# A constant product written into each free PSUM bank ahead of the real products of RWKV's blocks, retention and GLA

## The chip, the cores and the metric

The kernel runs on one core of a Trainium2 chip. A core has a matrix engine (TensorE: PE in the profile, PEld for its weight loads), VectorE (DVE), ScalarE (ACT), GpSimd (POOL), SyncE (SP, which only issues and waits here) and 16 DMA engines. The metric is the device time of one execution in microseconds. The kernel before takes 2861.12 us (median of 3 runs, 2857.55 to 2868.86).

## The reference

One encoder layer over 2048 tokens of width 1024, in float32: a norm, one input projection, four token mixers of width 256 side by side (retention, RWKV-7, a linear recurrence, gated linear attention), an output projection with a residual, a router that gives each of 16 experts its best 256 tokens, the experts' feed-forward products, and a last norm. The mixers are bidirectional. Cut to what the change touches:

```
def _retention_chunked(q, k, v, log_gamma):           # and the same on flipped inputs
    scores = einsum('bnihd,bnjhd->bnhij', qc, kc) * dmask
    y_intra = einsum('bnhij,bnjhe->bnihe', scores, vc)
    state = state * chunk_decay + kv_i                 # scan over chunks
    y_cross = einsum('bnihd,bnhde,hi->bnihe', qc, prev, xi)
...
def step(S, inp):                                      # RWKV-7, per token
    sa = einsum('bhvk,bhk->bhv', S, -kk_t)
    S = S * w_t + sa * (kk_t * a_t) + v_t * k_t
    y = einsum('bhvk,bhk->bhv', S, r_t)
...
def _gla_chunked(q, k, v, log_alpha):
    scores = where(lower, einsum('bnihk,bnjhk->bnhij', q_dec, k_dec), 0.0)
    y_intra = einsum('bnhij,bnjhv->bnihv', scores, v)
    S = S * dec + kv_i                                 # scan over chunks
```

## The kernel before

The program runs in stages. Until about 836 us the input projection runs, and beside it the linear recurrence and the first half of RWKV (`rwkv_a`: decays, and the inverses of the small triangular systems). From 836 to about 1450 us three streams share the engines, and this is the stage that the change touches: the rest of RWKV (`rwkv_rest`), retention and GLA. Then come the output projection of the remaining blocks (to about 1630 us), the choice of tokens (`top_k`) and the 16 experts (to the end).

RWKV's rest goes over 16 blocks of 128 tokens in both directions. For each block and direction `rwkv_prep` makes the block's matrices in six steps: transposes of two tensors (L606, then L615, with the identity as one operand), the products L628 (64 partitions, two banks), L639, L648, and L656 in two halves of two heads each. ScalarE or VectorE takes each bank to SBUF before the next step. One block later `rwkv_chain` does the recurrence (L672, two products of four heads per block and direction). Retention goes over 16 blocks of 128 tokens: transposes (L938), scores (L952), and the block's output (L960 and L963, accumulated in one bank), besides state updates (L909) in a first pass over all blocks and again in each. GLA goes over 16 blocks: two score products (L1217) and the output (L1233, L1234, L1236 in one bank), after a first pass that makes its decays.

Every product writes a PSUM bank from `bank`. PSUM has eight banks in three pools: four for RWKV's rest (stream 0), two for retention (stream 1), two for GLA (stream 2). A bank is handed to the next product when the last reader of its former contents is done. When RWKV's blocks are through, stream 0 goes on with the weights of the output projection (`out_weights`, L43 and L44) and with its first four blocks (`out_proj`, L129).

The streams are generators that a function weaves together, in shares of 100 for RWKV's rest, 56 for retention and 68 for GLA. This gives every instruction its priority. A scheduler then fixes the order on each engine ahead of time, by its own model of times: it takes an instruction when its operands are there and, if the instruction is the first to write a tile, when a buffer of the pool is free. On the chip each engine runs its list in that order.

In the profile a product of two float32 operands appears as two records, and a transpose as one.

Of the kernel before, what the change touches and what calls it, by code (L numbers as in the profile page):

```python
# [8 lines left out]
BF16 = mybir.dt.bfloat16  # L9
# [8 lines left out]
P = 128  # L18
# [27 lines left out]

def bank(g, which=None, shape=(P, 512)):
    return g.ps[g.stream if which is None else which].tile(list(shape), F32, name="bank", tag="bank")


def rstd_of(g, pool, ss, n, scale, eps, name):
# [510 lines left out]
def turn(ring):  # L562
    ring[1] += 1
    return ring[0][(ring[1] - 1) % len(ring[0])]
# [20 lines left out]
def rwkv_prep(g, dr, b, loaded, res):  # L585

    nc, c = g.nc, g.c
    ld, q1, ti = loaded  # L590
    q0 = turn(g.q0)
    z, v = ([ld[:, HALF * q + o:HALF * q + o + P] for q in range(2)] for o in (384, 512))
    bk = [[ld[:, HALF * q + 192 - 128 * e:HALF * q + 320 - 128 * e] for e in range(2)] for q in range(2)]
    R = g.bp.tile([P, NH, P], F32, name="R", tag="R")
    mv = [g.mp.tile([P, NH, C], F32, name=f"mv{e}", tag=f"mv{e}") for e in range(2)]
    g.mv[dr, b] = mv
    H = [slice(0, 64), slice(64, 128)]

    def qh(x):
        return x.rearrange("p (q h) c -> p q h c", q=2)  # L600

    p1 = bank(g)
    for q in range(2):
        for e in range(2):
            o = (2 * q + e) * P
            nc.tensor.transpose(p1[:, o:o + P], bk[q][e], c["ident"])  # L606
    p1 = p1.rearrange("p (q e h c) -> p q e h c", q=2, e=2, h=2)
    for e in range(2):
        for s, q in ((H[e], q0), (H[1 - e], q1)):
            nc.scalar.activation(out=qh(q[s, :, e, H[1 - e]]), in_=p1[s, :, e], func=AF.Copy)  # L610
    yield
    p2 = bank(g)
    for i, x in enumerate((z, v)):
        for q in range(2):
            nc.tensor.transpose(p2[:, i * 256 + q * P:i * 256 + (q + 1) * P], x[q], c["ident"])  # L615
    p2 = p2.rearrange("p (i h c) -> p i h c", i=2, h=NH)
    for e in range(2):
        nc.scalar.activation(out=R[H[e], :, H[e]], in_=p2[H[e], 0], func=AF.Copy)
        nc.scalar.activation(out=mv[e][H[1 - e]], in_=p2[H[1 - e], 1], func=AF.Copy)
    yield  # L620
    rd = turn(g.rd)
    for k in range(2):
        nc.vector.tensor_copy(out=rd[H[k], :, k], in_=ld[H[k]].rearrange("p (u t) -> p u t", t=320)[:, :, 0:C])
    pss = [bank(g) for _ in range(2)]
    for q in range(2):
        for k in range(2):
            ks = ld[H[k], HALF * q:HALF * q + 384].rearrange("p (u t) -> p u t", t=C)[:, 1::3]
            nc.tensor.matmul(pss[k][:, q * P:(q + 1) * P], lhsT=z[q][H[k]], rhs=ks, start=True, stop=True)  # L628
    for k in range(2):
        pv = pss[k][:, 0:256].rearrange("p (q e t) -> p q e t", q=2, e=2)  # L630
        for e in range(2):
            s = H[e]
            nc.vector.tensor_tensor(out=R[s, k::2, H[1 - e]], in0=pv[s, :, 1 - e], in1=c["m_bm"][s, dr, None, :].broadcast_to([64, 2, C]), op=OP.mult)
    yield
    ps = bank(g)
    for q in range(2):
        for e in range(2):
            o = (2 * q + e) * P
            nc.tensor.matmul(ps[:, o:o + P], lhsT=bk[q][e], rhs=rd[:, 2 * q + 1 - e], start=True, stop=True)  # L639
    pv = ps.rearrange("p (q e h t) -> p q e h t", q=2, e=2, h=2)  # L640
    for e in range(2):
        for s, q in ((H[e], q0), (H[1 - e], q1)):
            nc.vector.tensor_tensor(out=qh(q[s, :, e, H[e]]), in0=pv[s, :, e], in1=c["m_in"][s, dr, None, None, :].broadcast_to([64, 2, 2, C]), op=OP.mult)
    yield

    ps = bank(g)
    for h in range(NH):
        nc.tensor.matmul(ps[:, h * P:(h + 1) * P], lhsT=ti[:, h], rhs=R[:, h], start=True, stop=True)  # L648
    X = g.bp.tile([P, NH, P], F32, name="X", tag="X")
    nc.scalar.activation(out=X, in_=ps.rearrange("p (h c) -> p h c", h=NH), func=AF.Copy)  # L650
    yield
    E = g.ep.tile([P, NH, 2, P], F32, name="E", tag="E")
    for h2 in range(2):
        ps = bank(g)
        for h in range(2):
            nc.tensor.matmul(ps[:, h * 256:(h + 1) * 256], lhsT=X[:, 2 * h2 + h, :], rhs=q0[:, 2 * h2 + h].rearrange("p e c -> p (e c)"),  # L656
                             start=True, stop=True)
        s = slice(2 * h2, 2 * h2 + 2)
        nc.vector.tensor_tensor(out=E[:, s].rearrange("p h e c -> p (h e c)"), in0=q1[:, s].rearrange("p h e c -> p (h e c)"), in1=ps, op=OP.subtract)
        yield  # L660
    res[dr, b] = E
# [222 lines left out]
def retention(g):  # L884
# [44 lines left out]
    for j in range(NB // 4):  # L929
        y4 = g.sh.tile([P, 4, 256], F32, name="rt_y4")  # L930
        for b in range(4 * j, 4 * j + 4):
            ld = pool.tile([P, 768], F32, name="rt_ld")
            nc.sync.dma_start(out=ld, in_=g.tm[b, :, 0:768])
            vv = ld[:, 512:768]
            rot = rotate(g, pool, b, ld[:, 0:512], 2 * NH).rearrange("p h t -> p (h t)")
            ps = bank(g)
            for q in range(4):
                nc.tensor.transpose(ps[:, q * P:(q + 1) * P], rot[:, q * P:(q + 1) * P], c["ident"])  # L938
            pq = ps[:, 0:256].rearrange("p (q t) -> p q t", q=2)
            qd = turn(qds)  # L940
            for k in range(2):
                nc.scalar.activation(out=qd[halves[k], :, k], in_=pq[halves[k]], func=AF.Copy)
            qT = pool.tile([P, 2, P], F32, name="rt_qT")
            nc.scalar.activation(out=qT, in_=pq, func=AF.Copy)
            qs = pool.tile([P, 2, 2, P], F32, name="rt_qs")
            nc.gpsimd.tensor_tensor(out=qs, in0=qT[:, None].broadcast_to([P, 2, 2, P]), in1=g.rxi, op=OP.mult)
            kT = pool.tile([P, 2, P], F32, name="rt_kT")
            nc.scalar.activation(out=kT, in_=ps[:, 256:512].rearrange("p (q t) -> p q t", q=2), func=AF.Copy)
            sd = [diag(S[0]), diag(SB[:, b])]
            ps = bank(g)  # L950
            for q in range(2):
                nc.tensor.matmul(ps[:, q * 256:(q + 1) * 256], lhsT=kT[:, q], rhs=qd[:, q].rearrange("p k t -> p (k t)"), start=True, stop=True)  # L952
            sT = pool.tile([P, NH, P], F32, name="rt_sT")
            nc.vector.tensor_tensor(out=sT, in0=ps.rearrange("p (h t) -> p h t", h=NH), in1=g.rdt, op=OP.mult)
            yield
            ps = bank(g)
            for q in range(2):
                o = ps[:, q * P:(q + 1) * P]
                for e in range(2):
                    nc.tensor.matmul(o, lhsT=qs[:, e, q], rhs=sd[e][:, q].rearrange("p k v -> p (k v)"), start=(e == 0), stop=False)  # L960
                for h in (2 * q, 2 * q + 1):
                    s = slice(h * HD, (h + 1) * HD)
                    nc.tensor.matmul(ps[:, s], lhsT=sT[:, h], rhs=vv[:, s], start=False, stop=(h == 2 * q + 1))  # L963
            nc.scalar.activation(out=y4[:, b - 4 * j], in_=ps[:, 0:256], func=AF.Copy)
            if b + 1 < NB:
                state(0, b, rot[:, 256:512].rearrange("p (h t) -> p h t", h=NH), vv)
            yield
        head_norm(g, g.sh, y4.rearrange("p b (h v) -> p (b h) v", v=HD), 16, True, EPS)
        yield
        gated_out(g, g.sh, y4, j, 6, g.w_ret_gn, 0)  # L970
        yield
# [110 lines left out]
def gla(g):  # L1082
# [114 lines left out]
    for j in range(NJ):  # L1197
# [7 lines left out]
        for b in range(GB * j, GB * j + GB):  # L1205
# [5 lines left out]
            pss = []  # L1211
            for e in range(2):
                qx = pool.tile([P, NH, P], F32, name="gl_qx", tag="gl_qx")
                nc.gpsimd.tensor_tensor(out=qx, in0=o[:, 0, e, None, s].broadcast_to([P, NH, P]),
                                        in1=c["gl_hq"][:, :, None].broadcast_to([P, NH, P]), op=OP.mult)
                ps = bank(g)
                nc.tensor.matmul(ps, lhsT=o[:, 1, e, s], rhs=qx.rearrange("p h t -> p (h t)"), start=True, stop=True)  # L1217
                pss.append(ps.rearrange("p (h t) -> p h t", h=NH))

# [3 lines left out]
            for e in range(2):  # L1223
                p, r = H64[e], H64[1 - e]
# [3 lines left out]
            for p in H64:  # L1228
                nc.gpsimd.tensor_tensor(out=sT[p, :, p], in0=sT[p, :, p], in1=t[p], op=OP.add)
            yield  # L1230
            ps = bank(g)
            y = ps[:, 0:256]
            nc.tensor.matmul(y, lhsT=o[:, 0, 0, s], rhs=sx[0], start=True, stop=False)  # L1233
            nc.tensor.matmul(y, lhsT=o[:, 0, 1, s], rhs=sx[1], start=False, stop=False)  # L1234
# [591 lines left out]
```

## Time and profile before

| | us |
|---|---|
| median of 3 runs | 2861.12 |
| the profiled execution | 2858.58 |
| its span, first to last instruction | 2856.6 |
| PE busy | 2594.7 (91%) |
| PEld busy | 2321.6 (81%) |
| DVE busy | 1746.1 (61%) |
| ACT busy | 1392.3 (49%) |
| POOL busy | 711.5 (25%) |
| mean granted TensorE clock | 0.947 |

Busy time of PE includes the time that a product is in flight, so consecutive products overlap in it, and the distance of their starts tells better what one costs. The granted clock is the share of TensorE's full speed that the chip gave. It has two levels, 2.4 GHz (1.0) and 1.2 GHz (0.5), and a mean between them is a mixture over time.

### The profile page before, as it was taken

What the parts mean: (1) busy time and instruction counts of PE and PEld (TensorE: products, weight loads), DVE (VectorE), ACT (ScalarE), POOL (GpSimd) and SP (SyncE); (2) the same over time, 40 slices, a digit from 0 to 9 for tenths busy, and PEclk for the clock granted to TensorE, in tenths of its full rate; (3) what the DMA queues carried; (4) which work ended last, traced back from release to release, by engine and by line L of the source; (5) the groups of instructions that cost most, each with busy time, mean ns of one, the idle gap of its engine ahead of it and who ended that gap; (6) DMA issues with size and microseconds to landing.
All of it is one profiled execution on the core that took longest, in us unless ns stands there. A gap on an engine that the chain in (4) does not pass through costs nothing.

```text
span 2856.6 us, 47428 instructions
## 1 busy us (share of the span) xinstructions
PE 2594.7 (91%) x18433; PEld 2321.6 (81%) x18433; DVE 1746.1 (61%) x3415; ACT 1392.3 (49%) x2348; POOL 711.5 (25%) x771
## 2 busy tenths in 40 slices
PE   6989998989888888886979859999999999999997
PEld 5866787768767777774767659999999999999987
DVE  4454567766887667788443475555555555566564
ACT  4366555435434676555533334444444444455453
POOL 0011115443524454347433200000000000000121
PEclk9999999999988889997989979999999999999999
DMA  8735554675446544446344346666666666789873
GB/s 304 278 101 190 182 164 151 203 231 166 136 122 177 161 153 148 145 127 190 107 143 171 127 147 206 205 206 205 206 205 205 205 206 206 228 289 298 266 238 140
DMA packets 474015, 538.40 MB, mean 188 GB/s; under 512 B 129952, under 2 KB 411584, under 8 KB 473024
## 3 DMA queue, kind: packets, MB, share of 16 engines
q1 hardware_dynamic: 461984, 492.12, 53.3%
q0 software_dynamic: 11808, 43.26, 5.8%
q8 instruction: 145, 2.38, 0.3%
q14 instruction: 78, 0.64, 0.1%
HBM read 392.17 MB, written 145.23 MB: 188 GB/s over the span
## 4 chain that ended last, share of the span: by engine, by line
PE 53%; DVE 5%; DMA 4%; ACT 3%; issue 2%; POOL 1%; SPq 0%; POOLq 0%; ACTq 0%; DVEq 0%
PE bank L129 43%; DMA rt_ld<-tm 1%; PE bank L656 1%; PE bank L1500 1%; PE bank L639 1%; DMA fn_x<-acc,x_idx 1%; PE bank L628 1%; PE bank L672 1%; PE bank L1481 1%; PE bank L648 1%; DVE tk_j L1395 0%; PE bank L1217 0%; PE bank L1323 0%; PE bank L960 0%; PE bank L952 0%
## 5 line engine op out<-in xcount | busy, mean ns | idle before, releaser
L44 DVE TENSOR_TENSOR x_wl<-x_st,x_wh 128x2048 fp32r<-128x2048 f32 x192 | 439.5, 2292 | 306.3 <-ACT x_wh L43 305.9
L129 PE MATMUL bank<-x_xh,x_wh 128*128 128x256 f32 x2048 | 580.2, 285 | 2.9 <-ACT x_wh L43 2.8
L129 PE MATMUL bank<-x_xl,x_wh 128*128 128x256 f32 x2048 | 577.4, 283 | 0.0
L129 PE MATMUL bank<-x_xh,x_wl 128*128 128x256 f32 x2048 | 572.2, 283 | 1.1 <-DVE x_wl L44 1.1
L43 ACT ACTIVATE x_wh<-x_st 128x2048 fp32r<-128x2048 f32 x192 | 367.0, 1913 | 106.7 <-PE bank L129 96.6
L129 PEld LDWEIGHTS bank<-x_xh,x_wh 128*128 128x128 f32 x2048 | 393.2, 192 | 3.6 <-ACT x_wh L43 3.2
L129 PEld LDWEIGHTS bank<-x_xl,x_wh 128*128 128x128 f32 x2048 | 393.3, 192 | 0.0
L129 PEld LDWEIGHTS bank<-x_xh,x_wl 128*128 128x128 f32 x2048 | 389.9, 192 | 1.5 <-DVE x_wl L44 1.5
L129 PE MATMUL bank<-x_wh,x_hh 128*128 128x256 f32 x1024 | 290.1, 285 | 4.8 <-ACT x_hh L43 4.8
L129 PE MATMUL bank<-x_wl,x_hh 128*128 128x256 f32 x1024 | 291.2, 285 | 0.0
L129 PE MATMUL bank<-x_wh,x_hl 128*128 128x256 f32 x1024 | 289.8, 284 | 0.0
L1626 POOL DMA_INDIRECT acc<-x_os,x_idx x30 | 48.9, 1631 | 926.8 <-ACT x_os L1560 899.0
L129 PE MATMUL bank<-h_hi,w_hi 128*128 128x512 f32 x576 | 238.5, 417 | 20.1 <-DVE o_cm L1676 13.8
L129 PE MATMUL bank<-h_lo,w_hi 128*128 128x512 f32 x576 | 240.0, 417 | 0.0
L129 PE MATMUL bank<-h_hi,w_lo 128*128 128x512 f32 x576 | 235.6, 409 | 0.0
L129 PEld LDWEIGHTS bank<-x_wh,x_hh 128*128 128x128 f32 x1024 | 196.6, 193 | 5.0 <-ACT x_hh L43 5.0
L129 PEld LDWEIGHTS bank<-x_wl,x_hh 128*128 128x128 f32 x1024 | 197.4, 193 | 0.0
L129 PEld LDWEIGHTS bank<-x_wh,x_hl 128*128 128x128 f32 x1024 | 197.2, 193 | 0.0
L129 PE MATMUL bank<-w_hi,h_hi 128*128 128x256 f32 (+1 forms) x512 | 156.4, 306 | 14.6 <-DVE o_tm L1676 11.8
L129 PEld LDWEIGHTS bank<-h_hi,w_hi 128*128 128x128 f32 x576 | 112.5, 196 | 56.3 <-DVE o_cm L1676 16.4
L129 PE MATMUL bank<-w_lo,h_hi 128*128 128x256 f32 (+1 forms) x512 | 149.4, 292 | 0.0
L129 PE MATMUL bank<-w_hi,h_lo 128*128 128x256 f32 (+1 forms) x512 | 148.8, 291 | 0.0
(457 smaller groups left out, 5490.2 us busy)
## 6 DMA issues: line engine op xcount, KB each, us to landing
x_st<-in_exp_w_gate_dram SPq DMA_DIRECT2D x64, 1024.0 KB, 8.4
x_st<-in_exp_w_up_dram SPq DMA_DIRECT2D x64, 1024.0 KB, 8.9
x_st<-in_exp_w_down_dram SPq DMA_DIRECT2D x64, 1024.0 KB, 5.5
w_st<-in_w_in_dram SPq DMA_DIRECT2D x20, 1024.0 KB, 6.7
rw_sp<-sp SPq DMA_DIRECT2D x16, 1280.0 KB, 4.6
bld<-rw_sp SPq DMA_DIRECT2D x32, 640.0 KB, 4.1
ld<-rw_cm SPq DMA_DIRECT2D x14, 899.5 KB, 6.1
cm<-o_cm SPq DMA_DIRECT2D x40, 256.0 KB, 2.8
```

The source lines that it names most:

```text
L43: g.nc.scalar.activation(out=hi, in_=src, func=AF.Copy)
L44: (g.nc.gpsimd if pool else g.nc.vector).tensor_tensor(out=lo, in0=src, in1=hi.bitcast(F32), op=OP.subtract)
L129: g.nc.tensor.matmul(out, lhsT=lhs[a][:, k, lsl], rhs=rhs[b][:, k, rsl], start=(k + i == 0 and out is outs[0]), stop=(3 * k + i == 3 * nk ...
L628: nc.tensor.matmul(pss[k][:, q * P:(q + 1) * P], lhsT=z[q][H[k]], rhs=ks, start=True, stop=True)
L639: nc.tensor.matmul(ps[:, o:o + P], lhsT=bk[q][e], rhs=rd[:, 2 * q + 1 - e], start=True, stop=True)
L648: nc.tensor.matmul(ps[:, h * P:(h + 1) * P], lhsT=ti[:, h], rhs=R[:, h], start=True, stop=True)
L656: nc.tensor.matmul(ps[:, h * 256:(h + 1) * 256], lhsT=X[:, 2 * h2 + h, :], rhs=q0[:, 2 * h2 + h].rearrange("p e c -> p (e c)"), start=True ...
L672: nc.tensor.matmul(ps[:, h, :], lhsT=E[:, h, e, :], rhs=mv[e][:, h, :], start=True, stop=True)
L1481: nc.tensor.matmul(ps[:, 2 * s:2 * s + 2], lhsT=oh[:, i, s * P:(s + 1) * P], rhs=tok[:, i], start=(i == 0), stop=(i == NB - 1))
L1500: nc.tensor.transpose(ps[:, m * CAP + s * P:m * CAP + (s + 1) * P], xs[:, s, (k + m) * P:(k + m + 1) * P], c["ident"])
L1626: g.nc.gpsimd.indirect_dma_start(out=dst, out_offset=bass.IndirectOffsetOnAxis(ap=idx[:, s:s + 1], axis=0), in_=t[:, s], in_offset=None, **kw)
```

## The change

A new function `full` puts one product into a bank before the bank goes to its real user: the first 128 columns of the identity matrix, read as bf16, against 512 columns of the same matrix, over all 128 partitions and all 512 columns of the bank. Nothing reads its result: each real product starts its sum anew and writes over it. It stands ahead of L606, L615, the first of the two banks of L628, L639, L648 and both halves of L656 in RWKV's blocks; ahead of L938, L952 and L960 in retention; and ahead of both L1217 and of L1233 in GLA. The recurrence (L672), the state updates (L909), the first pass of GLA and the output projection are left as they are. Line numbers after the new function are higher by 8.

```
+def full(g, ps):
+    i = g.c["ident"].bitcast(BF16)
+    g.nc.tensor.matmul(ps.rearrange("p (a b) -> p a b", a=2), lhsT=i[:, 0:P], rhs=i[:, None, :].broadcast_to([P, 2, 2 * P]), start=True, stop=True)
+    return ps
...
@@ rwkv_prep
-    p1 = bank(g)
+    p1 = full(g, bank(g))
...
-    p2 = bank(g)
+    p2 = full(g, bank(g))
...
-    pss = [bank(g) for _ in range(2)]
+    pss = [full(g, bank(g)), bank(g)]
...
-    ps = bank(g)
+    ps = full(g, bank(g))
     for q in range(2):
         for e in range(2):
...
-    ps = bank(g)
+    ps = full(g, bank(g))
     for h in range(NH):
         nc.tensor.matmul(ps[:, h * P:(h + 1) * P], lhsT=ti[:, h], rhs=R[:, h], start=True, stop=True)
...
     for h2 in range(2):
-        ps = bank(g)
+        ps = full(g, bank(g))
...
@@ retention: three times, ahead of the transposes, the scores and the output
-            ps = bank(g)
+            ps = full(g, bank(g))
...
@@ gla: ahead of each score product and of the output
-                ps = bank(g)
+                ps = full(g, bank(g))
```

The scheduler places 320 such products on PE; 245 of them stand directly ahead of their own real product, and 75 have other products in between. The other products change places too. Two places show it.

The first is PE in RWKV's third block, from the products L648 (R times ti, both directions) to the end of L656 (q0 times X, both directions). Before:

```order
L648 MATMUL bank_8124<-R_7940,ti0_7184 128x128 x4
L648 MATMUL bank_8131<-R_7952,ti1_7185 128x128 x4
L909 MATMUL bank_7819<-rt_ld_7810,rt_kz_7817 128x128 x2
L656 MATMUL bank_8161<-q00_7166,X_8129 128x256 x2
L656 MATMUL bank_8166<-q01_7167,X_8136 128x256 x2
L656 MATMUL bank_8243<-q00_7166,X_8129 128x256 x2
L656 MATMUL bank_8247<-q01_7167,X_8136 128x256 x2
```

The same place of the change, the part with L656 (now L664; L55 is the constant product, whose weight load is a row of its own):

```order
L55 LDWEIGHTS c_ident_84
L55 MATMUL bank_8199<-c_ident_84 128x512
L664 MATMUL bank_8199<-q00_7166,X_8166 128x256 x2
L55 LDWEIGHTS c_ident_84
L55 MATMUL bank_8205<-c_ident_84 128x512
L55 LDWEIGHTS c_ident_84
L55 MATMUL bank_8283<-c_ident_84 128x512
L664 MATMUL bank_8283<-q00_7166,X_8166 128x256 x2
L664 MATMUL bank_8205<-q01_7167,X_8174 128x256 x2
L55 LDWEIGHTS c_ident_84
L55 MATMUL bank_8288<-c_ident_84 128x512
L664 MATMUL bank_8288<-q01_7167,X_8174 128x256 x2
```

Four constant products have come in, the bank of the second direction's first half (8205) is taken two products before its real use, and the halves of the first direction now follow each other.

The second place is PE at the end of RWKV's recurrence, the last product of L672 and what stands around it. Before:

```order
L938 MATMUL bank_10856<-c_ident_84,rt_a1_10851 128x128 x4
L1153 MATMUL bank_10818<-c_ident_84,gl_p_10297 128x128 x2
L672 MATMUL bank_12780<-mv1_12551,E_12697 128x64 x4
L672 MATMUL bank_12786<-mv0_12562,E_12702 128x64 x4
L952 MATMUL bank_10873<-rt_qd0_7362,rt_kT_10867 128x256 x2
L1159 MATMUL bank_10818<-gl_v_10299,gl_kt_10821 32x64 x8
```

And of the change (L672 is now L680, L938 is L946, L952 is L960):

```order
L680 MATMUL bank_13100<-mv1_12857,E_13013 128x64 x4
L946 MATMUL bank_11884<-c_ident_84,rt_a1_11879 128x128 x4
L680 MATMUL bank_13106<-mv0_12869,E_13019 128x64 x4
L960 MATMUL bank_11902<-rt_qd1_7369,rt_kT_11896 128x256 x2
```

Counted over the whole list, 10 of retention's 16 score products and 8 of GLA's 16 blocks stand ahead of that last product before, and 13 and 12 of the change: retention and GLA have moved forward against RWKV.

## Rows read from the trace of the kernel before

**Rows 1.** The page: granted TensorE clock in 40 slices, in tenths.
```profile
PEclk9999999999988889997989979999999999999999
```

**Rows 2.** By window: us, busy of PE, PEld, DVE, ACT, POOL (count), clock, DMA, GB/s.
```profile
836.00:1290.00 454.00, 387.64 (x2699) 333.91 (x2698) 345.18 (x837) 267.21 (x680) 206.45 (x312) 0.89 0.51 151
1290.00:1450.00 160.00, 124.78 (x666) 94.99 (x664) 102.10 (x230) 80.16 (x182) 93.44 (x83) 0.85 0.44 141
2000.00:2100.00 100.00, 100.00 (x888) 99.91 (x887) 54.45 (x73) 46.18 (x56) 6.05 (x4) 1.00 0.64 202
```

**Rows 3.** The chain that ended last, shares by line, 836 to 1450 us.
```profile
by line: PE bank L129 5.7%; DMA rt_ld<-tm 5.0%; issue 4.6%; PE bank L656 4.5%; PE bank L639 4.5%; PE bank L628 3.8%; PE bank L672 3.5%; PE bank L648 2.3%; PE bank L1217 2.0%; PE bank L960 1.7%; PE bank L952 1.7%; DMA bld<-rw_sp 1.7%; DVE wo
```

**Rows 4.** Groups on PE, 836 to 1450: busy us, mean ns, idle before.
```profile
L656 PE MATMUL bank<-q,X 128*128 128x256 f32 x256 | 63.6, 399 | 12.5 <-ACT X L650 9.7 <-DVE q L643 2.7
L639 PE MATMUL bank<-rd,bld 128*128 128x128 f32 x256 | 42.4, 328 | 4.8 <-DVE R L633 4.5 <-ACT mv L619 0.3
L628 PE MATMUL bank<-bld 64*128 64x128 f32 x256 | 40.6, 369 | 11.6 <-DVE R L633 6.9 <-ACT yt L680 3.2 <-ACT mv L619 1.1
L1217 PE MATMUL bank<-gl_qx,gl_p 128*128 128x512 f32 x64 | 36.9, 660 | 11.3 <-DVE gl_t L1227 5.2 <-POOL rt_kz L906 2.0 <-POOL rt_a L879 1.6
L648 PE MATMUL bank<-R,ti 128*128 128x128 f32 x256 | 35.7, 288 | 2.4 <-issue 2.4
...
L615 PE MATMUL bank<-c_ident,bld 128*128 128x128 f32 x128 | 22.5, 318 | 5.7 <-ACT q L610 5.6
L960 PE MATMUL bank<-rt_sd,rt_qs 128*128 128x128 f32 x128 | 21.8, 295 | 0.0
...
L952 PE MATMUL bank<-rt_qd,rt_kT 128*128 128x256 f32 x64 | 19.2, 424 | 3.4 <-ACT rt_kT L948 3.4
L606 PE MATMUL bank<-c_ident,bld 128*128 128x128 f32 x128 | 18.9, 283 | 9.5 <-DMA bld<-rw_sp 8.4 <-DVE E L659 1.1
...
L938 PE MATMUL bank<-c_ident,rt_a 128*128 128x128 f32 x64 | 11.8, 316 | 2.6 <-POOL rt_a L880 2.6
L1233 PE MATMUL bank<-gl_sx,gl_p 128*128 128x256 f32 x32 | 11.3, 438 | 8.7 <-DVE gl_t L1227 8.2 <-ACT gl_sT L1225 0.4
```

**Rows 5.** PE in order of time: start us, us, line, product, count.
```profile
1246.86 1.10 PE L1217 MATMUL bank<-gl_qx,gl_p 128*128 128x512 f32 x2 [0.19 <-DVE gl_t L1227]
1247.79 2.75 PE L656 MATMUL bank<-q,X 128*128 128x256 f32 x12
```

**Rows 6.** The same around 1016 us; in brackets idle time and releaser.
```profile
1016.49 2.04 PE L628 MATMUL bank<-bld 64*128 64x128 f32 x12 [2.72 <-DVE R L633]
...
1019.37 3.30 PE L639 MATMUL bank<-rd,bld 128*128 128x128 f32 x16
1022.50 1.00 PE L672 MATMUL bank<-mv,E 128*128 128x64 f32 x8
```

**Rows 7.** By window around that wait, columns as in rows 2.
```profile
1012.00:1015.40 3.40, 1.34 (x10) 0.91 (x8) 1.33 (x4) 2.74 (x5) 2.11 (x7) 0.99 0.67 210
1015.40:1022.20 6.80, 5.71 (x30) 5.37 (x31) 4.22 (x14) 4.40 (x14) 5.11 (x5) 0.50 0.28 95
```

**Rows 8.** Waits of PE, 836 to 1450: us in total, times, longest.
```profile
PE bank L656 <- ACT X L650: 9.7, 5, 3.1
PE bank L606 <- DMA bld<-rw_sp: 8.4, 2, 4.2
...
PE bank L628 <- DVE R L633: 6.9, 3, 3.5
PE bank L615 <- ACT q L610: 5.6, 6, 2.0
```

**Rows 9.** Retention's scores after 1288 us: ns min/median/max, first and last start.
```profile
L952 PE MATMUL bank<-rt_qd,rt_kT x22: 377/379/795, 1287.8 to 1441.1; 128*128 128x256 f32 x22
```

**Rows 10.** GLA's scores after 1288 us, the same view.
```profile
L1217 PE MATMUL bank<-gl_qx,gl_p x32: 590/592/1190, 1291.2 to 1437.0; 128*128 128x512 f32 x32
```

**Rows 11.** RWKV's recurrence, 836 to 1450 us, the same view.
```profile
L672 PE MATMUL bank<-mv,E x512: 219/275/475, 870.6 to 1287.2; 128*128 128x64 f32 x171
```

More of the change, by code (lines that the diff above doesn't have):

```diff
@@ L955, in retention @@
             yield
-            ps = bank(g)
+            ps = full(g, bank(g))
             for q in range(2):
@@ L1215, in gla @@
                                         in1=c["gl_hq"][:, :, None].broadcast_to([P, NH, P]), op=OP.mult)
-                ps = bank(g)
+                ps = full(g, bank(g))
                 nc.tensor.matmul(ps, lhsT=o[:, 1, e, s], rhs=qx.rearrange("p h t -> p (h t)"), start=True, stop=True)
@@ L1230, in gla @@
             yield
-            ps = bank(g)
+            ps = full(g, bank(g))
             y = ps[:, 0:256]
```

## The prediction

> **What bounds the kernel now.** I read the clock by slices first. It stands at 9 or more nearly everywhere, and falls to 7 or 8 in the middle and at the end of the mixers' stage [rows 1]. The second view is busy time by window for that stage: from 836 to 1290 us PE is busy 387.6 of 454 us at a mean clock of 0.89, DVE 345.2; from 1290 to 1450 us PE is busy 124.8 of 160 at 0.85 [rows 2]. So PE is the fullest engine there, but not full: it idles 66 + 35 = 101 of 614 us. The clock has two levels, so 0.89 means that 22% of the first stretch, 100 us, ran at 1.2 GHz, and 0.85 means 30% of the second, 48 us. Third is the chain that ended last over the 614 us: nine PE lines in its row make up 5.7 + 4.5 + 4.5 + 3.8 + 3.5 + 2.3 + 2.0 + 1.7 + 1.7 = 29.7%, the rest is spread over DMA, ACT and DVE in small pieces [rows 3]. What is added to PE there is therefore partly on the path. Fourth are PE's waits. The longest kinds have two different causes. L656 waits for X from ACT and L606 for a DMA: operands. L628 waits for DVE's R and L615 for ACT's q: these read the bank that the product wants, so these are waits for a bank [rows 8].
>
> **What the change adds.** The counts of the groups give the sites: 256 records of L656 are 64 banks; L639, L628 and L648 with 256 each are 32; L615 and L606 with 128 are 32; L938 and L952 with 64 and L960 with 128 are 16; L1217 with 64 is 32; L1233 with 32 is 16 [rows 4]. That is 64 + 5 x 32 + 3 x 16 + 32 + 16 = 320 products of 512 columns in bf16, each with a weight load.
>
> **The price of one.** No row has a bf16 product of this size. From below: in the experts' stretch PE starts 888 records of mostly 256 columns in 100 us, which is 0.113 us for 256 columns and 0.225 us for 512 [rows 2]. From above: the two records of a float32 product of 512 columns take 0.93 us from 1246.86 to 1247.79, 0.465 us each [rows 5]. I take 0.225, since one pass over 512 columns is what is issued, and keep 0.465 as the other end. The weight load is costed at nothing: PEld runs beside PE all over this stage (333.9 us of 454 [rows 2]), and if that cover is gone a load could add some 0.1 us, which the upper end holds. At the lower clock all of this doubles. At 0.225 the 320 come to 72 us.
>
> The Trainium skill, page TensorE: Matmul & The Clock Gate, section Back-to-back issue gap, gives about 131 ns for a product of 512 columns in a sustained stream. By that figure the path term below would be 19 us instead of 32 and the time about 2860. The trace does not agree: its densest stretch gives 225 ns for as many columns, and that is what I use.
>
> **How many lie on the path.** The chain's shares, times 614 us, against the same lines' busy time: L656 27.6 of 63.6 us, L639 27.6 of 42.4, L628 23.3 of 40.6, L648 14.1 of 35.7, L1217 12.3 of 36.9, L960 10.4 of 21.8, L952 10.4 of 19.2 [rows 3, 4]. Together that is 125.7 of 260.2 us, 48%. For the four lines that the chain's row does not name I take the same share (their bound is 10.4 us each, the smallest named). So 154 products are on the path: 34.7 us at the full clock, and as 148 of 614 us ran at half, 24% of them cost double: 43 us. A product that runs while PE waits for an operand is free, and one that waits for the bank itself is not: it starts when the bank comes free, and the real one comes after it. Of the waits in view the first kind has 18.1 us (X, and the DMA of bld) and the second 12.5 [rows 8], but there are few of them, and most of PE's idle time lies in short gaps. I let a quarter of the products be hidden (none and a half are the bounds): 43 - 11 = 32 us, with bounds of 21 and 43; at 0.465 us a product it would be 66.
>
> **What the clock gives back.** Of the 148 us at half speed, 29.7% lie on PE in the chain: 44 us, of which 22 return if the clock never falls. How a fall looks: from 1012 to 1015.4 us PE is busy 1.34 of 3.40 us at 0.99, and the next 6.8 us are granted 0.50; the product that waited 2.72 us is an L628 that DVE's R releases, and the 16 records of L639 at 1019.37 then take 3.13 us to the next start [rows 6, 7]. One constant product adds 0.225 us to such a window, and in this one it would wait for the same bank. I expect it to help where the window was nearly busy enough, and while the clock is low, where each of them fills twice the time. I take 10 us, with 0 and 22 as the bounds.
>
> The Trainium skill speaks against even that. The same page, section A second HAM failure mode: psum-queue depth-cycling, says that PE's short idles between groups of products that cycle through banks bring the clock down and up again. The trace agrees (0.99, then 0.50 after a wait for a bank, in the two windows just named). Products that need the very banks cannot close these gaps then, and the third rival below is what that makes of the time.
>
> **What moves.** Ahead of the recurrence's last product the order now has three more blocks of retention and four more of GLA. Before, 22 records of L952 (5.5 blocks) and 32 of L1217 (8 blocks) start after 1288 us [rows 9, 10], the recurrence having ended at 1287.2 [rows 11], and the stretch behind has 35 us of PE idle [rows 2]. With about half of those blocks done earlier this stretch shortens. What goes over is PE work of 3 x 3.3 + 4 x about 3 = 22 us, from a stretch with 22% idle into one with 15%. If all idle goes the gain is 35 us; if the moved work finds the first stretch full, while the tail is held by its DVE and DMA work, it is a loss of about 10. I take a gain of 10.
>
> **Sum.** 32 - 10 - 10 = +12 us on the profiled execution's 2858.6, which is 2870.6. The median of the runs shown is 2.5 above that execution, so the forecast is 2873. About 0.5% (14 us) is what a measurement of this kernel can tell from no change, and the forecast lies just inside that.
>
> **Rivals.**
> - The clock holds and the tail closes, so the kernel gets faster. For it: 148 us at half speed, and a tail in which PE idles 22%. Against it: the falls follow waits for banks. Full clock gives 22, the tail 33: 32 - 22 - 33 = -23, so 2838.
> - Banks are taken too early, so it gets clearly slower. The order has 75 constant products with other products between them and their real one, 25 of these at L656 in RWKV's pool of four banks. A bank that is held for a product whose operand is late keeps the recurrence and the other direction out. Waits for banks last 5.6/6 = 0.93 us at L615 and 6.9/3 = 2.3 us at L628 [rows 8]; 25 times 0.93 is 23 us on top of the forecast: 2896. It decides once more than about half of those early claims end in such a wait. Against it: three of four constant products (245) stand next to their own.
> - The clock gives nothing back: the falls come from waits for banks (L628, L615 [rows 8]), and a product into the same bank starts after the wait. 32 - 0 - 10 = +22, so 2883. For it: the bank that L628 waits for at 1016.49. Against it: at half speed each constant product fills 0.45 us of PE, which should bring the rise forward in places.
> - Nothing comes of it: PE's idle time takes all 72 us of products (there are 101), and the clock stays as it is. Then 2861. Against it: half of PE's lines lie on the chain.
>
> **How the numbers follow.** The forecast gets 0.32, the faster case 0.26, early claims 0.18, the clock that gives nothing 0.14, no effect 0.10. The forecast's own range is 2862 to 2882 (the path's 21 to 43 us with half of the clock's 0 to 22 against it), somewhat less of it beyond the 0.5% bound at 2875 than below: 0.10 slower, 0.22 same. The faster case spreads over 2825 to 2852, 0.22 of it beyond the bound at 2847 and 0.04 same. Early claims are slower, the unmoved clock too but for 0.01, and no effect is the same. That makes faster 0.22, same 0.37, slower 0.41. The range reaches from the middle of the faster case, 2838, to that of the early claims, 2897; about 0.2 is left out.
>
> **What would show it.** In the profile after, 320 records on the new line with starts 0.22 to 0.24 us apart from what follows at the full clock; more than that says the price is wrong. PE's busy time from 836 us to the end of the stage grows by some 70 us. The mean clock from 836 to 1450 us should be around 0.92; at 0.96 or more the faster case is the right one, at 0.89 the clock term was nothing. The last recurrence product should start some 35 to 50 us later than 1287, and the distance from there to the stage's end should be shorter than the 163 us to 1450. Long waits of L672 or of constant products for banks that ACT or DVE had not emptied would speak for early claims. The forecast is wrong if the stage's end moves by more than 25 us either way, or if the stages before 836 or after 1630 us change at all.

## The result, and the profile after

The changed kernel takes 2883.63 us (median; 2881.24 to 2884.56) against 2861.12 before: a difference of 22.5 us. The ratio over the runs of both kernels is 1.0068, with a 95% interval of 1.005 to 1.0085, which is 19.5 us, between 14 and 24. One of its five runs took 11078 us and is left out of the comparison as disturbed. I take 19.5 us as the cost of the change, and costs by ratio in all that follows; the forecast was 12. The profiled execution after took 2884.56 us, with a span of 2882.5 (before 2858.58 and 2856.6).

The page after shows the clock in 40 slices and the busy row of PE. It answers to [rows 1]:

```profile
PE 2643.7 (92%) x18753; PEld 2343.7 (81%) x18753; DVE 1767.3 (61%) x3415; ACT 1389.8 (48%) x2346; POOL 709.5 (25%) x771
...
PEclk9999999999999998999899969999999999999998
```

The slices below 9 in the middle are fewer than before (three instead of seven, one of them deeper), and the mean clock of the execution rose from 0.947 to 0.962. PE is busy for 49 us more. So the clock was held up, and the kernel is slower all the same.

To see where the time went I cut the stage at two instants: the last recurrence product (1287.2 us before, 1360.8 after) and the last router product of the output projection (1628.8 and 1648.9). The first real product of RWKV's blocks starts at the same time within 0.1 us (841.1 and 841.2). First the two stretches of before by window, then those of after; the columns are those of [rows 2]:

```profile
841.00:1287.00 446.00, 383.80 (x2660) 330.79 (x2660) 338.78 (x828) 260.49 (x664) 200.15 (x300) 0.89 0.51 150
1287.00:1629.00 342.00, 292.68 (x1601) 223.83 (x1600) 173.39 (x469) 143.74 (x298) 154.91 (x156) 0.90 0.43 145
841.00:1629.00 788.00, 676.48 (x4258) 554.62 (x4258) 512.17 (x1296) 404.23 (x961) 355.06 (x456) 0.89 0.47 148
```

```profile
841.00:1361.00 520.00, 467.88 (x3149) 380.54 (x3149) 378.49 (x890) 292.65 (x747) 230.24 (x337) 0.93 0.47 139
1361.00:1649.00 288.00, 259.69 (x1427) 199.22 (x1426) 155.72 (x408) 108.79 (x214) 120.38 (x118) 0.96 0.46 155
841.00:1649.00 808.00, 727.57 (x4574) 579.76 (x4574) 534.21 (x1297) 401.45 (x959) 350.62 (x454) 0.94 0.47 144
...
836.00:1450.00 614.00, 535.18 (x3481) 429.02 (x3480) 455.23 (x1026) 336.21 (x834) 290.52 (x389) 0.92 0.49 146
```

Subtract length and busy time. Up to the recurrence's end the stretch is 74 us longer: PE is busy 84 us more and idle 10 us less (52 instead of 62). Behind it the stretch is 54 us shorter: PE is busy 33 us less and idle 21 us less (28 instead of 49). Over the stage that is +20 = +51 busy - 31 idle. The rest of the program after the stage is 5.6 us longer in this execution, with no line of it changed. I take that for its scatter, since the runs give 19.5 in all, and since over the profiled executions of all kernels here that rest lies between 1227 and 1234 us (1228 before).

Next the lines' own rows (ns min/median/max, first and last start), which answer to [rows 9 to 11]. After the change all line numbers are 8 higher: L672 is L680, L952 is L960, L1217 is L1225.

```profile
L55 PE MATMUL bank<-c_ident x320: 376/379/634, 836.4 to 1436.6; 128*128 128x512 bf16 x160
...
L680 PE MATMUL bank<-mv,E x512: 219/275/453, 869.1 to 1360.8; 128*128 128x64 f32 x171
...
L960 PE MATMUL bank<-rt_qd,rt_kT x64: 379/379/792, 1005.2 to 1417.5; 128*128 128x256 f32 x64
...
L1225 PE MATMUL bank<-gl_qx,gl_p x64: 590/592/1061, 1122.2 to 1433.6; 128*128 128x512 f32 x64
```

There are 320 constant products, as counted; 301 of them start before 1361 us, 297 of these after 841. The last score product of retention and GLA starts at 1433.6 us instead of 1441.1, only 73 us behind the recurrence's last product instead of 154. What starts late instead is the output projection's first four blocks: their first product comes at 1419.9 us instead of 1352.8, so they no longer lie beside retention and GLA.

PE in order of time after shows the price (start us, us in flight, product, count; in brackets idle time and its releaser):

```profile
1089.84 0.38 PE L55 MATMUL bank<-c_ident 128*128 128x512 bf16 x1
1090.05 1.03 PE L664 MATMUL bank<-q,X 128*128 128x256 f32 x4
...
1094.68 0.38 PE L55 MATMUL bank<-c_ident 128*128 128x512 bf16 x1
1094.90 0.60 PE L623 MATMUL bank<-c_ident,bld 128*128 128x128 f32 x4
1097.60 0.59 PE L55 MATMUL bank<-c_ident 128*128 128x512 bf16 x1 [2.10 <-ACT q L618]
1097.98 1.06 PE L623 MATMUL bank<-c_ident,bld 128*128 128x128 f32 x4
```

From a constant product's start to the next start are 0.21 to 0.22 us at the full clock (the median of all 320 is 216 ns), and 0.43 at half (a median of 427 ns over those that start there). The 0.38 in the row is time in flight, not the price. The last two rows show the other half of the matter: the constant product itself waits 2.10 us for a bank that ScalarE still reads, and the real one follows it. The two windows around that wait after, like [rows 7] before, with the clock as the third number from the right:

```profile
1096.60:1097.90 1.30, 0.30 (x1) 0.18 (x1) 0.29 (x1) 1.29 (x5) 0.98 (x1) 0.80 0.00 0
1097.90:1107.00 9.10, 9.10 (x39) 6.87 (x38) 4.42 (x12) 8.18 (x21) 4.45 (x11) 0.50 0.17 58
```

So such a wait still ends in half speed. PE's waits from 836 to 1480 us after (total, times, longest) show that waits ahead of a constant product are common; they answer to [rows 8]:

```profile
PE bank L55 <- DVE q L651: 11.8, 11, 2.3
PE bank L786 <- DVE rw_y L89: 8.3, 3, 7.4
PE bank L946 <- POOL rt_a L888: 5.0, 4, 3.6
PE bank L664 <- ACT X L658: 4.4, 2, 2.4
PE bank L55 <- DVE gl_t L1235: 4.1, 3, 2.6
PE bank L55 <- DVE R L641: 4.0, 3, 2.4
```

The waits for a bank that stood at L628 and L615 (for DVE's R, 6.9 us, and ACT's q, 5.6) now stand at L55, with 4.0 and 3.5 us. The largest at L55, 11.8 us for the q that DVE takes from a bank, is mostly new: before, L656 waited 2.7 us for it. The chain that ended last from 836 to 1475 us, by line, answers to [rows 3]:

```profile
by line: PE bank L55 6.1%; DMA rt_ld<-tm 5.7%; issue 5.4%; PE bank L664 5.1%; PE bank L137 4.6%; DVE q L651 3.7%; PE bank L680 3.3%; PE bank L636 2.8%; PE bank L647 2.7%; PE bank L1225 2.6%; PE bank L656 2.6%; DVE pr L492 2.0%; DVE R L641 1
```

L55 leads it: 6.1% of 639 us, 39 us.

### The profile page after: what moved, and what is told of

It reads as the page before. It is cut to its first block, busy times and chain, and to the rows that moved or that the text cites. A ratio compares the mean times of both kernels' runs of the same rounds, so it can differ in the third digit from the quotient of the medians.

```text
span 2882.5 us, 47912 instructions
## 1 busy us (share of the span) xinstructions
PE 2643.7 (92%) x18753; PEld 2343.7 (81%) x18753; DVE 1767.3 (61%) x3415; ACT 1389.8 (48%) x2346; POOL 709.5 (25%) x771
## 4 chain that ended last, share of the span: by engine, by line
PE 57%; DVE 14%; DMA 8%; ACT 5%; issue 5%; POOL 3%; SPq 1%; POOLq 0%; DVEq 0%; ACTq 0%
PE bank L137 45%; DMA ld<-rw_cm 3%; PE bank L55 1%; DMA rt_ld<-tm 1%; PE bank L664 1%; DVE x L493 1%; PE bank L1508 1%; DMA fn_x<-acc,x_idx 1%; DVE q L651 1%; POOL pr L492 1%; PE bank L680 1%; DVE pr L492 1%; PE bank L636 1%; PE bank L647 1%; PE bank L1225 1%
## 5 line engine op out<-in xcount | busy, mean ns | idle before, releaser
L137 PE MATMUL bank<-w_hi,h_hi 128*128 128x256 f32 (+1 forms) x512 | 155.3, 303 | 14.1 <-DVE o_tm L1684 11.7
L55 PE MATMUL bank<-c_ident 128*128 128x512 bf16 x320 | 122.5, 402 | 37.8 <-DVE q L651 11.8
```

The costliest lines, as they stand in the source:

```text
L55: g.nc.tensor.matmul(ps.rearrange("p (a b) -> p a b", a=2), lhsT=i[:, 0:P], rhs=i[:, None, :].broadcast_to([P, 2, 2 * P]), start=True, sto ...
L137: g.nc.tensor.matmul(out, lhsT=lhs[a][:, k, lsl], rhs=rhs[b][:, k, rsl], start=(k + i == 0 and out is outs[0]), stop=(3 * k + i == 3 * nk ...
```

## The experiments

All but one of the runs change which products there are or their shape; each such kernel gets its own order from the scheduler. All were timed in five rounds against the kernel before. In the table "PE added" is the number of constant products times their distance to the next start at the full clock. "Half speed" is the time at 1.2 GHz from the first constant or real product of RWKV's blocks, retention and GLA to the last router product, counted from the profiled execution of each kernel; before it is 167 us. "Recurrence" is the start of its last product.

| run | PE added | half speed | recurrence | ratio [95%] | us |
|---|---|---|---|---|---|
| the change | 69 | 96 | 1361 | 1.0068 [1.005, 1.0085] | +19.5 |
| e1_narrow | 9 | 174 | 1326 | 1.0008 [0.9991, 1.0025] | +2.3 |
| e2_rwkv_only | 48 | 137 | 1343 | 1.0081 [1.006, 1.0103] | +23.2 |
| e3_ret_gla_only | 21 | 126 | 1312 | 0.9994 [0.9977, 1.0011] | -1.7 |
| e4_rwkv_first | 69 | 137 | 1323 | 1.0117 [1.0096, 1.0138] | +33.5 |
| e5_rwkv_ends | 21 | 147 | 1308 | 1.0008 [0.9996, 1.002] | +2.3 |
| e6_rwkv_middle | 28 | 99 | 1324 | 0.9998 [0.9987, 1.0008] | -0.6 |
| e7_half_rows | | 99 | 1381 | 1.0193 [1.0169, 1.0216] | +55.3 |
| e8_two_each | 138 | 89 | 1438 | 1.0202 [1.0188, 1.0215] | +57.8 |
| e9_half_width | 35 | 99 | 1300 | 0.997 [0.996, 0.998] | -8.6 |
| e10_ret_gla_two | 41 | 123 | 1329 | 1.0034 [1.002, 1.0049] | +9.7 |
| e11_middle_ret_gla | 48 | 125 | 1330 | 1.0041 [1.0027, 1.0056] | +11.7 |
| e12_quarter_width | 18 | 143 | 1312 | 1.0015 [1.0005, 1.0024] | +4.3 |

**Is it the order or the products?** The first run keeps every constant product, and so every early claim of a bank, but makes it 32 columns wide.

```
-    matmul(ps (2 x 256 columns), lhsT=i[:, 0:P], rhs=i twice)
+    matmul(ps[:, 0:32], lhsT=i[:, 0:P], rhs=i[:, 0:32])
```

> All 320 constant products stay, but each has 32 columns instead of 512. Theory A (the cost is the time that the products take on PE, less what the clock gives back): a product of 32 columns takes at most about 0.06 us, 48% of 320 on the path make under 9 us, and the clock is held up less than with 512 columns; 2861 to 2869 us. Theory B (the cost is the order: banks claimed ahead, retention and GLA moved forward against RWKV): the order still has the products ahead of the same places and 12 and 10 blocks of retention and GLA ahead of the recurrence's end (10 and 8 before, 13 and 12 with 512 columns), so most of the 22 us stays; 2872 to 2883 us.

Its constant products and its recurrence (duration ns, first and last start), and the stage by window:

```profile
L55 PE MATMUL bank<-c_ident x320: 176/179/234, 838.8 to 1465.2; 128*128 128x32 bf16 x160
...
L680 PE MATMUL bank<-mv,E x512: 219/275/476, 875.5 to 1326.3; 128*128 128x64 f32 x171
```

```profile
844.00:1643.00 799.00, 711.20 (x4566) 584.79 (x4566) 527.75 (x1295) 404.46 (x961) 349.06 (x446) 0.89 0.47 146
```

The recurrence ends 39 us later than before and the kernel is not measurably slower. Only some of the shift is there (16 records of retention's scores and 24 of GLA's are left behind the recurrence; 24 and 32 before, 12 and 16 in the change). The clock stayed at 0.89. So early claims and a later recurrence cost next to nothing by themselves, and 32 columns return nothing.

The opposite test keeps the products and gives RWKV's stream a larger share, so that it runs ahead again:

```
-WR, WG = 100, 68
+WR, WG = 160, 68
```

> All 320 products at full width, but RWKV's rest has a share of 160 instead of 100 in the weave, so that 10 and 8.5 blocks of retention and GLA stand ahead of the recurrence's end, as before the change (10 and 8). Theory A: the products still take their time on PE and the clock is as high as in the change; 2876 to 2884 us. Theory B: the early blocks of the output projection lie beside retention and GLA again; 2858 to 2868 us.

```profile
L680 PE MATMUL bank<-mv,E x512: 219/275/477, 871.4 to 1322.7; 128*128 128x64 f32 x171
```

The recurrence ends 38 us earlier than in the change, with 24 and 30 records left behind it, and the kernel is slower by another 14 us: the last score product of retention starts at 1488.7 us. Theory B, that early claims and the recurrence's later end are what costs, falls twice. The order is not free for that. E4 has the change's products in another order, and besides the 14 us it has 41 us more at half speed and, as before, a long wait of the transposes of a mixer's output (L983 before, L991 after) for the norm that VectorE makes, which the change has not. PE's longest wait in e4, and the two longest before (total, times, longest):

```profile
PE bank L991 <- DVE hn_t L67: 16.3, 1, 16.3
```

```profile
PE bank L983 <- DVE hn_t L59: 16.0, 1, 16.0
PE bank L1233 <- DVE gl_t L1227: 8.2, 1, 8.2
```

**Which sites?** Four runs leave constant products out by site. The lines are those of after.

```
e2: full(g, bank(g)) -> bank(g)  in retention and GLA  (224 products left)
e3: the same                     in rwkv_prep          (96 left)
e5: only at p1 (L614) and L664   (96 left: the sites that mostly wait for an operand)
e6: only at L623, L636, L647 and L656  (128 left: the sites that mostly wait for a bank)
```

> Constant products only in RWKV's blocks, 224 of the 320. Theory A: 70% of the cost and of the clock's return, about +15, 2873 to 2879 us. Theory B: the order has 12 and 12 blocks of retention and GLA ahead of the recurrence's end, nearly as in the whole change, so nearly the whole cost: 2879 to 2884 us.

> Constant products only in retention and GLA, 96 of the 320. Theory A: 30% of the cost, about +6, 2863 to 2870 us. Theory B: 11 and 10.5 blocks stand ahead of the recurrence's end, half of the way moved; +5 to +11, and of the 96 products 39 claim their bank ahead of other products; 2866 to 2872 us.

> Constant products only ahead of L606 and L656 in RWKV's blocks, 96 of the 224 there: the real products that in the trace before waited for operands (X from ACT, a DMA). Theory A1 (each product costs its PE time wherever it stands): 96/224 of the 26 us that RWKV's products cost alone, +11, 2870 to 2877 us. Theory A2 (a product costs where the real one waited for the bank, and is free where it waited for operands): 2860 to 2866 us.

> Constant products only ahead of L615, L628, L639 and L648 in RWKV's blocks, 128 of the 224: the real products that in the trace before waited mostly for their bank. Theory A1: 128/224 of 26 us, +15, 2874 to 2882 us. Theory A2: nearly all of the 26 us, 2882 to 2890 us.

The parts do not add up: the ends cost 2, the middle nothing, both together (e2) 23 us, above both ranges named for it. The sites that wait for banks were to be the dear ones by theory A2; they are free, and A2 falls. Their stage by window goes with that:

```profile
844.00:1632.00 788.00, 686.21 (x4385) 549.63 (x4383) 528.47 (x1299) 405.07 (x964) 347.50 (x457) 0.94 0.48 148
```

128 products raise the clock to 0.94, as far as the change's 320 do, for two fifths of the PE time. Two more runs ask whether the place (RWKV dear, retention and GLA free: theory P) or the amount decides:

```
e10: two constant products at each place of retention and GLA, none in RWKV (192)
e11: the places of e6 and of e3 together (224, as many as e2)
```

> Two constant products at each place in retention and GLA and none in RWKV, 192 in all, 41 us of PE time. Theory A1 (the amount decides): 20 minus some 8, +12, 2872 to 2880 us. Theory P (the place decides, and retention and GLA are off the path): -5 to +3, 2858 to 2867 us.

> Constant products ahead of L615, L628, L639 and L648 in RWKV's blocks and everywhere in retention and GLA, 224, as many as in RWKV alone, which cost 23 to 26 us. Theory A1: 48 us of PE time, 23, less what the clock gives back, 8 to 11 since both parts alone kept the clock up: +12 to +15, 2874 to 2880 us. Theory P (L606 and L656 together with the rest of RWKV make the cost): +0 to +5, 2862 to 2869 us.

Both cost 10 to 12 us. Doubling the free places of retention and GLA makes them dear, so P in its pure form falls. Whether the amount does that or the order is not separated: e10 has a wait of 19.7 us at the transposes named above, e3's is 12.4. The same 224 products cost 23 us in e2 and 12 in e11, which the amount alone does not explain; the half-speed time does not either (137 and 125 us, some 4 us by the fit below). What else differs is PE's waits of over 6 us: e2 has three, 28.6 us together, the longest the row below, and e11 one of 8.6.

```profile
PE bank L991 <- DVE gl_y L89: 14.8, 1, 14.8
```

**Which amount?** Two runs go up from the change: twice as many products, and products over 64 rows instead of 128.

```
e8: for _ in range(2): matmul(...)            (640 products)
e7: lhsT=i[0:64, 0:P], rhs=i[0:64] twice      (512 columns, half of the rows)
```

> Two constant products ahead of each real one, 640 in all. Theory A1: the second 72 us of PE time cost as the first or more, since less of PE's idle time is left and less half-speed time is left to give back; 2900 to 2930 us. If the cost were one of order or of the claim on the bank (once per bank, as in the change): 2880 to 2892 us.

> All 320 products at 512 columns, but over 64 of the 128 partitions: as long on PE, half of the array at work. If the granted clock goes by the time that PE streams: as the change, 2879 to 2887 us, half-speed time in the mixers' stage as in the change (some 95 us). If it goes by the part of the array at work: the half-speed time goes back towards the 150 us before, and the time is 2887 to 2900 us.

The stage of e8, and then that of e7, by window:

```profile
842.00:1691.00 849.00, 783.47 (x4886) 599.97 (x4890) 520.30 (x1298) 399.38 (x958) 346.40 (x453) 0.95 0.45 137
```

```profile
845.00:1688.00 843.00, 776.52 (x4574) 561.15 (x4574) 522.76 (x1295) 406.45 (x962) 350.70 (x456) 0.94 0.45 138
```

E8 adds 69 us of PE to the change, lowers half-speed time by 7 us and costs 38 us more. E7 has the change's clock and leaves as many records behind the recurrence (12 and 16), has 49 us more of busy PE, and costs 36 us more. Where the clock hardly improves any more, added PE time is paid at 0.55 (e8, by the distance of starts) and 0.73 (e7, by busy time).

Two runs go down in width:

```
e9:  matmul(ps[:, 0:256], lhsT=i[:, 0:P], rhs=i)
e12: matmul(ps[:, 0:128], lhsT=i[:, 0:P], rhs=i[:, 0:128])
```

> All 320 products with 256 columns instead of 512, so 35 us of PE time instead of 69. Theory A1 (48% of the added PE time is paid, and 0.15 us comes back for each us less at half speed): 17 minus some 8, +9, 2869 to 2877 us. Theory S (the first 30 us or so of added PE time are free since PE idles, as the runs with 96 and 128 products suggest, and all beyond is paid): +2 to +5, 2862 to 2869 us.

> All 320 products with 128 columns, some 18 us of PE time. Theory A1 with both terms taken from the runs so far (0.61 us for each us of added PE time, less 0.34 us for each us less at half speed in the mixers' stage, which fits the eleven runs to about 4 us): 11 us are paid, and half-speed time between that with 32 columns (174 us) and that with 256 (99 us), about 125, gives back 14; -3, 2854 to 2862 us. Theory O (the gain with 256 columns came from its own order and not from the clock): the order here is another one, with 12 and 10 blocks ahead of the recurrence's end as with 32 columns, and the time is that of 32 columns plus the added PE time; 2865 to 2873 us.

The constant products of e9 (ns, first and last start) and its stage by window, then the stage of e12:

```profile
L55 PE MATMUL bank<-c_ident x320: 269/273/421, 836.6 to 1433.2; 128*128 128x256 bf16 x160
```

```profile
842.00:1622.00 780.00, 688.75 (x4574) 556.65 (x4572) 530.80 (x1297) 402.17 (x961) 348.02 (x455) 0.94 0.48 150
```

```profile
842.00:1627.00 785.00, 697.34 (x4574) 570.50 (x4574) 526.52 (x1302) 402.07 (x962) 350.27 (x457) 0.91 0.48 149
```

With 256 columns the stage reaches the clock of the change, 0.94, at half of its PE time, and is 8 us shorter than before. The kernel takes 2851.93 us and beats both: 0.997 of the kernel before [0.996, 0.998]. With 128 columns the clock comes only half of the way, 0.91, and the kernel is a little slower than before. That landed in the range of theory O, by which e9's gain would be its own order; but the half-speed time that the other theory presumed did not come either, and with the measured one it allows +3 (measured +4.3). So whether e9 gains by its clock alone or also by its order stays open; that it has no wait of over 6 us, where the kernel before has the two shown above, speaks for a part of the order.

Of the twelve expectations four named a range that the time fell into (e1, e5, e8, e12). Six times lie outside both ranges, e2, e4 and e7 above them, e3, e6 and e9 below, and those of e10 and e11 between the two.

**The two terms together.** A least-squares fit over the change and ten of the runs (without e7, whose price is different, and e12, which came later) gives: time = 0.61 of the PE time added, less 0.34 of the half-speed time saved. The residuals have a root mean square of 3.8 us; the largest are -6.7 (e9) and +5.8 (e6). For the change it reads 0.61 x 69 = 42 us paid and 0.34 x 72 = 24 given back, +18. This is a fit over kernels with different orders, with half-speed times from one execution each: it says how large the two terms are, not more. One thing that differs with the order is in neither term: PE's single waits of over 6 us, 24 us in all before, 7 in the change, 29 in e2, none in e9. With them as a third term the fit is 0.64 of the PE time added, less 0.29 of the half-speed time saved, less 0.34 of what these waits fall by; the residuals fall to 2.2 us, and e9's gain would be that of its lost waits (8 us). That is a hint only: it hangs on where the line is drawn (at 3 us the third factor is 0.15 and the residuals 3.6), and no run changes such a wait alone.

## Why the prediction was right, and where its terms were not

The forecast of 2873 us was 11 us short; the time lies in the range, and slower had the largest of the three chances. Of the sum 32 - 10 - 10 the price held and no term did: by the windows of the two profiled executions the three come to 59 - 18 - 21 = +20. The misses partly cancelled, so that the time fell into the range is in part luck.

- **The price** was right: 0.216 us measured, 0.225 taken. The upper end of 0.465 was not needed. The Trainium skill, page TensorE: Matmul & The Clock Gate, section Back-to-back issue gap, has 131 ns for 512 columns in a sustained stream; no row here comes near it.
- **The path term** was mis-sized: 32 us against 59 by the windows (69 us added, 10 of idle time taken up to the recurrence's end), or about 42 by the fit, which has no term for what moves. The step that failed is in the stretch before the recurrence's end. There 297 products make 64 us, 52% of them and a quarter of the rest were costed at nothing, and idle time gave 10 of its 62 us, to them and to the blocks of retention and GLA that moved there. The group of L55 from 836 to 1480 us shows where (busy us, mean ns, then idle time before it):

```profile
L55 PE MATMUL bank<-c_ident 128*128 128x512 bf16 x320 | 122.5, 402 | 37.8 <-DVE q L651 11.8 <-DVE gl_t L1235 4.1 <-DVE R L641 4.0
```

  A constant product is the first writer of a bank and inherits the wait for it, 37.8 us in all. Where the bank is what the real product waited for too, it starts when PE could have started the real product, and delays it by its whole price. The text had named that case, but gave it only part of the gaps. How many of the 320 are of that kind no run counts.
- **The clock term** was mis-sized too: 10 us against 24 by the fit, and 18 by the windows (69 us added, 51 busy; a change in how products overlap is in that too). Half-speed time fell from 167 to 96 us: up to the recurrence's end from 99 to 72, behind it from 68 to 23. The second part can hardly be the constant products' own work: 19 of the 320 lie there. Before, 41 of its 68 us are two stretches at half speed around the two long waits shown above (by window, the clock again third from the right):

```profile
1305.50:1326.00 20.50, 9.64 (x42) 6.97 (x43) 18.40 (x28) 9.68 (x18) 15.57 (x10) 0.50 0.58 175
1448.90:1469.40 20.50, 6.05 (x18) 4.83 (x19) 11.65 (x31) 6.22 (x7) 6.00 (x4) 0.50 0.57 181
```

  In the order of the change neither wait is left (the longest behind the recurrence is 7.4 us), and no constant product stands at L983. The first part, in a stretch that is longer by 74 us, holds 301 of the 320 products. The mean of 0.92 from 836 to 1450 us is what the prediction named for its own case. So the third rival, whose 2883 the time happens to equal, is wrong by its mechanism: the clock did give something back. The limit that the text saw is real: falls after waits for banks remained (the one at 1097.60 us).
- **What moves**: the stretch behind the recurrence did close, by 54 us, of it 21 in idle time; the 10 us forecast there were too few. One wait, the 16.0 us at L983, was a third of the idle time there, and the prediction had not looked at it. The recurrence itself came 74 us later, not 35 to 50. The last router product came 20 us later, inside the 25 that the prediction allowed. The output projection's first blocks lost their cover beside retention and GLA, which no step had named. In e1 part of the shift came at no measurable price, and in e4 undoing it cost 14 us; a gain from it was not shown.
- **Early claims** fall with e1, which has them and no measurable cost. **Nothing comes of it** falls with the ratio. **The faster case** did not come with this width; its mechanism may be what carries e9. (It took 33 us for the tail where the rows give 35, which makes its sum -25.)
- **PE busy** was to grow by about 70 us; it grew by 51, and the higher clock is one reason: at 1.0 a constant product is 0.22 us from the next start, at 0.5 0.43. The stages before stayed unchanged; what comes after was 5.6 us longer in the profiled execution, where the prediction had allowed nothing.

## What to carry to other kernels

A product that only keeps PE going and is the first writer of a bank was paid here, by the fit, at more than half its PE time even though PE idles a seventh of the time (111 of 788 us before); it inherits the bank's wait and can delay the real product behind it. What it gives back through the clock does not grow with the amount: of 167 us at half speed 68 went with 128 products, 72 with 320 and 79 with 640, but only 31 with 224 (e2), and 31 with the same 320 in another order (e4). So the size is to be measured from small to large: half the width won 0.3% where the full width lost 0.7%, though the order may have a part in that. The order that the scheduler makes is itself worth as much as the change: 14 us between e4 and the change, 12 between e2 and e11. And a clock that rises in the profile is no gain by itself: set the busy time added against the half-speed time saved.

## What the hardware showed that I had not expected

**A product over 64 rows cost more than one over 128.** In e7 the constant products are in flight as long as in the change (ns, first and last start, then idle time before them, whose first entry is 9.5 us, 33 times in the change). Its PE in order of time:

```profile
L55 PE MATMUL bank<-c_ident x320: 372/386/631, 840.4 to 1465.1; 64*128 64x512 bf16 x160
its engine sat idle before it (us, times) until:
  issue: 42.2, 134
```

```profile
1202.79 0.28 PE L680 MATMUL bank<-mv,E 128*128 128x64 f32 x1
1203.00 0.39 PE L55 MATMUL bank<-c_ident 64*128 64x512 bf16 x1
1203.32 1.16 PE L656 MATMUL bank<-R,ti 128*128 128x128 f32 x8
...
1206.19 0.39 PE L55 MATMUL bank<-c_ident 64*128 64x512 bf16 x1
1206.51 0.71 PE L656 MATMUL bank<-R,ti 128*128 128x128 f32 x4
```

To the next start are 0.32 us (0.22 with 128 rows). From the start of a product of up to 128 columns before it are 0.21 (0.11 with 128 rows). It is the switch that costs, not the half height: L636, a real product over 64 rows, shows it the other way round. In the change it starts 0.31 us after a constant product of 128 rows, in e7 0.23 after one of 64:

```profile
896.83 0.38 PE L55 MATMUL bank<-c_ident 128*128 128x512 bf16 x1
897.14 0.71 PE L636 MATMUL bank<-bld 64*128 64x128 f32 x4
```

```profile
964.58 0.39 PE L55 MATMUL bank<-c_ident 64*128 64x512 bf16 x1
964.81 0.60 PE L636 MATMUL bank<-bld 64*128 64x128 f32 x4
```

So a switch between 64 and 128 rows costs about 0.1 us each way. In e7 243 of the 320 constant products have a product of 128 rows behind them and 247 have one before: some 49 us, which is what PE is busy for more than in the change. No run tells why.

**The same clock with half of the rows.** E7's stage was granted 0.94, as the change's was, while the 32 columns of e1 left it at 0.89. **And with few products:** the 128 of e6 came with 0.94 too, the 224 of e2 with 0.92. These are one profiled execution each, and no run tells why.
